# Zero blocks, lambda and position rows of the mixers' later parts, made behind the projection of the scan's inputs

## The chip, the cores and the metric

The kernel runs on one core of one Trainium2 chip. The metric is the device time of one execution in microseconds (us), as the median of several runs. The core has five engines that run their own queues in order and wait for each other by semaphores: PE (TensorE, matrix products), DVE (VectorE), ACT (ScalarE), POOL (GpSimd) and SP (SyncE, which here only issues DMAs). TensorE's granted clock has two levels, 1.2 and 2.4 GHz; the profile gives it as a share of the higher one.

## The reference, cut to what matters

Two request batches of 1024 rows and 1024 columns go through the same hybrid layer. One input projection feeds two mixers:

- Mixer A (RWKV-7): from columns r, k, v and three small groups (decay, learning rate, gate) comes a scan over time in both directions, with a matrix state of 64 x 64 for each of eight heads.
- Mixer B (differential attention): four heads with two halves each. The scores get a relative-position bias from a table of 32 buckets, and the second half's softmax is subtracted with a learned factor:

```
lam  = exp(sum(lp[0] * lp[1])) - exp(sum(lp[2] * lp[3])) + lam_init
attn = p[:, :, 0] - lam * p[:, :, 1]
```

The outputs of both are joined, projected, normalised, and go through a gated feed-forward part with a convolution of width three. All of it is float32; the dense products are made of three products of split values (a high and a low part of each operand).

## The kernel before

One core does both batches, and one program order is turned into five engine queues by a scheduler: each instruction has a priority (its place in the program, moved by the code), and of the instructions whose operands would be ready the scheduler takes the one of the best priority. The queues are fixed when the program is built; the chip only runs them.

`run` (L1138 on) lays the work out. The head is `consts`, the input norm of batch 0 (`norm_in`, with transposes into the two resident arrays `xh` and `xl`) and `columns`, which loads small parameters as rows and turns them into columns. Up to here priorities are the program's own. Then the dense code follows at a priority lowered by 100000: `project(0)` (14 column blocks of the input projection: block 12 with decay and rate, block 13 with the gate, then r, k, v for each of four pairs of heads), `project_qk(0)`, `project_v(0)`, `scan(0)`, then the same for batch 1, and the output and feed-forward parts. One column block is 48 products of 128x512 ("dense products" below: lines L264, L265, L266, and L288 to L290 for blocks in the other orientation). Beside `project(0)` and `project_qk(0)` the input norm of batch 1 runs (`between`).

`scan` stands late in the program but has a better priority (`self.first`) than all dense code, so its instructions go into the queues as soon as they can. It has three stages. `pass1` makes the scan's operands in 16 units (four pairs of heads, two halves of time, two directions): a decay product on PE (L549), tanh on ACT (L551), a running sum on DVE (L557), exponentials on ACT (L560, L562), the operand tile `AB` on DVE and POOL (L575, L576, L586, L587), a product of 32 small pieces on PE (L580), and stores. Every four units a triangular inversion runs on DVE (L619, L621, 30 pairs of small instructions), and two merges of its quarters run on PE (L647, L653) with copies on ACT, through DRAM scratch `td`. `pass2` is the chain of the scan itself (L724), and `attention` comes last. While `scan(0)` runs, the dense products of `project(1)` are released by its progress (`paced`), 50 us of them at once.

What the change touches stands at the end of `columns` (L195 to L226):

- the scratch `td` gets its zero blocks: a zero tile `zt` (DVE, L197) and eight DMAs from it (L201, issued by SP, each 1024 pieces of 128 bytes);
- lambda: a load, two DVE instructions (L206, L209), an exponential on ACT (L210), one DVE instruction (L211), one product on PE into a PSUM tile `pl` (L213), and a copy to `lamn` (L215);
- the position rows: a load of the bias table, 31 copies on POOL (L222), and two DMAs into the scratch `frow` (L225, L226).

`td` is read by `pass2` and written by `pass1`'s inversions; `lamn` and `frow` are read by `attention`. All small tiles come from the tag `t` (7 buffers), and `pl` comes from `spsum`, which hands out two tags, "a" and "b", in turn, each with two buffers:

```
def spsum(self, tag=None):
    self.side = not self.side
    return self.ps.tile([P, 512], F32, name=self.nm("s"), tag=tag or "ab"[self.side])
```

The tiles of a tag are handed out in the order in which the program asks for them. `pass1` asks for its products' tiles by the same function.

Of the kernel before, what the change touches and what calls it, by code (L numbers as in the profile page):

```python
# [42 lines left out]
class Trunk:  # L43
# [90 lines left out]
    def columns(self):  # L134

        nc, cp, I = self.nc, self.cp, self.I
# [55 lines left out]
        self.cb = cols[:, 300:344]  # L192
        self.rk = cols[:, rows["r_k"] : rows["r_k"] + 4]
        self.WC = self.cs.tile([P, NPAIR, 2, NC2, 2], F32, name="WC")
        self.td = [[self.scr(f"td{g}{h}", [P, 2, 2, NC2, C]) for h in range(2)] for g in range(2)]  # L195
        zt = self.dt("t", shape=(32, 4 * NC2, 32))
        nc.vector.memset(zt, 0.0)  # L197
# [940 lines left out]
    def run(self, x0, x1, y0, y1):  # L1138
        self.st = {}
        with self.tc.tile_pool(name="cs", bufs=1) as self.cs:  # L1140
            self.consts()
            for _ in self.norm_in(0, x0, True):
                pass
            self.columns()
            self.first_loads = self.loaded
            self.urgent = self.tc.cur_priority
            self.front = self.urgent + 30000
            self.first = self.urgent + 50000
            self.tc.cur_priority += 100000
            between = self.norm_in(1, x1)  # L1150
            self.project(0, between)
            self.project_qk(0, between)
            for g in range(2):
                turn = self.turn_in(1, g)
                next(turn)
                self.project_v(0, g)
                with self.ahead():
                    next(turn, None)
            self.scan(0)
            self.project(1)  # L1160
            self.project_qk(1)
            self.project_v(1, 0)
            self.project_v(1, 1)
            self.scan(1)
            with self.ahead():
                self.phase_o(0)
            self.phase_f1(0)
            self.phase_f2(0, y0)
            with self.tc.tile_pool(name="o1", bufs=1) as pool:
                self.phase_o(1, pool)  # L1170
        with self.tc.tile_pool(name="f1", bufs=1) as pool:
            h = pool.tile([P, KF, 2, 512], F32R, name="h")
            self.phase_f1(1, h)
            self.phase_f2(1, y1, h)
# [25 lines left out]
```

## Time and profile before

| | us |
|---|---|
| median of 3 runs (3603.18 to 3615.9) | 3606.48 |
| the profiled execution | 3613.08 |
| its span | 3611.3 |
| PE busy | 3254.0 (90%) |
| DVE busy | 1961.5 (54%) |
| ACT busy | 1379.4 (38%) |
| POOL busy | 1292.2 (36%) |

The span runs from the first to the last instruction that the profile shows; 1.8 us of the execution lie around it. A busy share is a mean over stages. In the timeline a row is one or several equal instructions: start, length, engine, line, operation, tiles; in square brackets the idle time of the engine before it and what ended that. A stretch of the span is written A:B, in us from its start.

### The profile page before, as it was taken

Reading aid. Unit: us, or ns where it says so; the run is one execution under the profiler, and the core shown is the slowest. Engines: PE = TensorE matmul, PEld = TensorE weight load, DVE = VectorE, ACT = ScalarE, POOL = GpSimd, SP = SyncE. Lnnn points to the kernel's source line nnn. Section 1 sums busy time; section 2 is a strip of 40 time slices with the busy share of each in tenths; the row PEclk is TensorE's granted clock in tenths of the full one; section 3 lists DMA queues with packets and bytes.
Section 4 is the critical chain, followed back from the end, with each engine's and each line's share of the span. In section 5 each row is a group of like instructions: output and inputs, shape, how many; then the busy total and the mean of one; then the engine's idle time right before and its main releaser. Section 6 shows DMA issues by size and latency. Waiting matters only on the chain. (4 is left out here: it accounts for less than half of the span.)

```text
span 3611.3 us, 56096 instructions
## 1 busy us (share of the span) xinstructions
PE 3254.0 (90%) x21477; PEld 2584.8 (72%) x21477; DVE 1961.5 (54%) x3550; ACT 1379.4 (38%) x2349; POOL 1292.2 (36%) x1387
## 2 busy tenths in 40 slices
PE   5788888998999986789999999989987899999997
PEld 4566666676777874567777787767865688888876
DVE  6378873335557866888534445366685633333022
ACT  3233332443245643345334343334454422332222
POOL 5365441001422445544121112363352622222464
PEclk9898888998999998788999999999999999999999
DMA  5568774534455655567543336586552322222642
GB/s 161 163 201 228 211 193 126 154 106 118 128 171 155 215 200 165 162 153 166 127 133 115 117 104 210 175 261 209 185 188 93 114 71 71 70 70 70 225 172 87
DMA packets 603360, 545.59 MB, mean 151 GB/s; under 512 B 205341, under 2 KB 477965, under 8 KB 603093
## 3 DMA queue, kind: packets, MB, share of 16 engines
q1 hardware_dynamic: 536532, 508.44, 46.3%
q10 hardware_dynamic: 66560, 33.56, 3.9%
q8 instruction: 171, 2.80, 0.3%
q14 instruction: 97, 0.79, 0.1%
HBM read 361.49 MB, written 180.39 MB: 150 GB/s over the span
## 5 line engine op out<-in xcount | busy, mean ns | idle before, releaser
L251 POOL TENSOR_TENSOR w<-w,whi 128x256 fp32r<-128x256 f32 (+1 forms) x800 | 758.6, 975 | 1246.1 <-ACT whi L248 1088.0
L264 PE MATMUL d<-xh,whi 128*128 128x512 f32 (+1 forms) x2112 | 863.7, 409 | 17.8 <-DVE t L399 6.0
L265 PE MATMUL d<-xl,whi 128*128 128x512 f32 (+1 forms) x2112 | 855.2, 405 | 0.6 <-DVE xl L308 0.6
L266 PE MATMUL d<-xh,w 128*128 128x512 f32 (+1 forms) x2112 | 853.7, 404 | 2.1 <-POOL w L251 2.1
L248 ACT ACTIVATE whi<-w 128x512 fp32r<-128x512 f32 (+1 forms) x536 | 307.9, 622 | 728.7 <-PE d L290 234.5
L264 PEld LDWEIGHTS d<-xh,whi 128*128 128x128 f32 (+1 forms) x2112 | 408.7, 194 | 117.3 <-issue 8.8
L266 PEld LDWEIGHTS d<-xh,w 128*128 128x128 f32 (+1 forms) x2112 | 407.9, 193 | 99.7 <-POOL w L251 3.3
L265 PEld LDWEIGHTS d<-xl,whi 128*128 128x128 f32 (+1 forms) x2112 | 408.2, 193 | 93.5 <-issue 2.0
L1071 DVE SCALAR_TENSOR_TENSOR t<-d,cols,t 128x1023 f32<-128x1023 f32 x88 | 112.8, 1282 | 455.7 <-ACT t L1070 442.6
L288 PE MATMUL d<-whi,xh 128*128 128x512 f32 x640 | 259.2, 413 | 31.5 <-DVE t L1051 15.1
L289 PE MATMUL d<-w,xh 128*128 128x512 f32 x640 | 259.2, 405 | 0.9 <-POOL w L251 0.9
L290 PE MATMUL d<-whi,xl 128*128 128x512 f32 x608 | 245.7, 404 | 0.0
L1051 DVE SCALAR_TENSOR_TENSOR t<-t,d 128x512 f32<-128x512 f32 x112 | 72.7, 678 | 244.7 <-PE d L290 240.7
L928 ACT ACTIVATE e<-e,ms 128x1024 f32<-128x1024 f32 x128 | 147.1, 1149 | 123.8 <-DVE ms L926 105.3
L935 POOL TENSOR_SCALAR e<-e,ms 128x512 f32<-128x512 f32 x128 | 88.1, 701 | 268.8 <-DVE ms L933 110.7
L288 PEld LDWEIGHTS d<-whi,xh 128*128 128x128 f32 x640 | 123.9, 194 | 66.7 <-DVE rs L1051 11.9
L739 DVE TENSOR_TENSOR G<-s,ms 64x256 f32<-64x256 f32 x128 | 53.4, 417 | 171.4 <-PE s L724 170.3
L289 PEld LDWEIGHTS d<-w,xh 128*128 128x128 f32 x640 | 124.0, 194 | 29.5 <-POOL w L251 2.2
L290 PEld LDWEIGHTS d<-whi,xl 128*128 128x128 f32 x608 | 117.2, 193 | 28.3 <-issue 1.0
L919 PE MATMUL s<-k,qh 128*128 128x512 f32 x256 | 113.9, 446 | 25.9 <-DVE ms L922 15.6
L619 DVE TENSOR_TENSOR Ntmp<-N 128x30 f32<-128x30 f32 (+14 forms) x240 | 111.3, 464 | 34.0 <-DMA N<-abd 29.0
L758 POOL COPY vr<-v 128x256 f32<-128x256 f32 x32 | 13.0, 405 | 324.4 <-DMA v<-va 311.3
(228 smaller groups left out, 5944.9 us busy)
## 6 DMA issues: line engine op xcount, KB each, us to landing
w<-in_ffn_up SPq DMA_DIRECT2D x88, 512.0 KB
w<-in_ffn_down SPq DMA_DIRECT2D x88, 512.0 KB
h<-t SPq DMA_DIRECT2D x66, 512.0 KB
ab<-AB ACTq DMA_DIRECT2D x64, 512.0 KB
w<-in_w_in SPq DMA_DIRECT2D x58, 512.0 KB
G<-ab SPq DMA_DIRECT2D x128, 128.0 KB
BK<-ab SPq DMA_DIRECT2D x64, 256.0 KB
w<-in_w_out SPq DMA_DIRECT2D x32, 512.0 KB
```

The lines of the kernel that those rows point to most:

```text
L248: nc.scalar.activation(out=hi[:, s], in_=w[:, s], func=AF.Copy)
L251: nc.gpsimd.tensor_tensor(out=lo[:, s], in0=w[:, s], in1=hi[:, s].bitcast(F32), op=ALU.subtract)
L264: nc.tensor.matmul(o, wh, rh, start=first, stop=False)
L265: nc.tensor.matmul(o, wh, rl, start=False, stop=False)
L266: nc.tensor.matmul(o, wl, rh, start=False, stop=last)
L288: nc.tensor.matmul(out[i], lh, wh, start=k == ks[0], stop=False)
L289: nc.tensor.matmul(out[i], lh, wl, start=False, stop=False)
L290: nc.tensor.matmul(out[i], ll, wh, start=False, stop=k == ks[-1])
L619: nc.vector.tensor_tensor(out=tv, in0=N[:, 0:j, j : j + 1].to_broadcast([P, j, w]), in1=N[:, j : j + 1, j + 1 : 32].to_broadcast([P, j, w] ...
L919: nc.tensor.matmul(pp, q_[0], k_[c][:, ks], start=True, stop=False)
L928: nc.scalar.activation(out=e_, in_=e_, func=AF.Exp, bias=ms[:, 2 + c : 3 + c], accum_out=ms[:, 4 + c : 5 + c])
L1071: nc.vector.scalar_tensor_tensor(out=o[:, 1:T], in0=pp[:, 0 : T - 1], scalar=self.cw[0][:, m : m + 1], in1=o[:, 1:T], op0=ALU.mult, op1=AL ...
```

## The change

The three groups at the end of `columns` become a function of their own, `tables`, with the same instructions, and `run` calls it behind `project(0)` instead of within `columns`. In the program they now stand behind `project(0)` and ahead of `project_qk(0)`, at the dense code's priority.

```diff
         self.WC = self.cs.tile([P, NPAIR, 2, NC2, 2], F32, name="WC")
+
+    def tables(self):
+
+        nc, cp, I = self.nc, self.cp, self.I
         self.td = [[self.scr(f"td{g}{h}", [P, 2, 2, NC2, C]) for h in range(2)] for g in range(2)]
         zt = self.dt("t", shape=(32, 4 * NC2, 32))
         nc.vector.memset(zt, 0.0)
...
             self.project(0, between)
+            self.tables()
             self.project_qk(0, between)
```

All five queues change from the head on until the first steps of `pass2` of batch 0. From about the 3000th of PE's 16822 products on, each engine's queue holds the same instructions in the same order as before.

On PE, before, at lambda's product (`s_419`; `d_544` is block 13, `d_624` block r of pair 0):

```order
L264 MATMUL d_544<-xh,whi_536 96x512
L265 MATMUL d_544<-xl,whi_536 96x512
L266 MATMUL d_544<-xh,w_537 96x512
L213 MATMUL s_419<-t_415,bcol 128x1
L264 MATMUL d_624<-xh,whi_616 128x512
```

Lambda's product stood here between blocks 13 and r, and the first decay product of `pass1` (`s_2584`) 43 rows further, within block r.

On PE, now, at the same two products (lambda's is `s_1478`; `d_1628` is the first k block of `project_qk(0)`, `stk_273` are the loaded decay rows):

```order
L269 MATMUL d_1628<-xl,whi_1620 128x512
L270 MATMUL d_1628<-xh,w_1621 128x512
L217 MATMUL s_1478<-t_1474,bcol 128x1
L553 MATMUL s_2584<-stk_273_2549,up_262_2521 128x512
L268 MATMUL d_1628<-xh,whi_1620 128x512
```

Both moved from within `project(0)` to the second block of `project_qk(0)`: 723 dense products now stand ahead of them, where 96 stood ahead of lambda's and 138 ahead of the decay product; the decay product asks for its tile next after lambda's in the same tag.

On SP, before, at the end of `columns` and in the first blocks of `project(0)` (`w` are weights, `stk` the decay and rate rows):

```order
L79 DMA td_401<-t_402 1024x1x32 x2
L79 DMA t_412<-in_lam 1x256
L79 DMA kk_2532<-in_iclr_up 128x1x512
L79 DMA kk_2539<-in_iclr_up 128x1x512
L79 DMA t_423<-in_rel_bias 4x32x1
L79 DMA frow<-t_425 4x1024
L79 DMA w_678<-in_w_in 128x8x128
L79 DMA stk_529<-t_525 4x32x1024 x2
L79 DMA stk_529<-t_526 4x32x1024 x2
L79 DMA frow<-t_426 4x1023
```

Here the weights `w_678` and the `stk` stores stood behind all of the zero blocks, lambda's load and the first half of the position rows.

On SP, now, at the same place:

```order
L79 DMA kk_2532<-in_iclr_up 128x1x512
L79 DMA kk_2539<-in_iclr_up 128x1x512
L79 DMA w_615<-in_w_in 128x8x128
L79 DMA w_679<-in_w_in 128x8x128
L79 DMA stk_466<-t_462 4x32x1024 x2
L79 DMA stk_466<-t_463 4x32x1024 x2
L79 DMA t_536<-in_g_up 96x512
L79 DMA stk_273_2549<-stk_466 128x512
```

The zero blocks, lambda's load and the position rows have left this place; the next weights and the `stk` stores follow the two loads of `in_iclr_up` directly. They stand again some fifty rows later, between the loads for the first blocks of `project_qk(0)`.

## Rows read from the trace of the kernel before

**Rows 1.** The page's first part: busy time of each engine.

```profile
PE 3254.0 (90%) x21477; PEld 2584.8 (72%) x21477; DVE 1961.5 (54%) x3550; ACT 1379.4 (38%) x2349; POOL 1292.2 (36%) x1387
```

**Rows 2.** Busy time by stretch: length, each engine's busy us, clock, DMA share, GB/s.

```profile
66.70:107.70 41.00, 13.61 (x45) 10.14 (x44) 11.49 (x14) 5.91 (x7) 13.18 (x39) 0.68 0.33 106
...
148.16:313.17 165.01, 147.04 (x738) 115.71 (x736) 124.80 (x172) 57.34 (x81) 92.50 (x93) 0.91 0.69 206
313.17:509.94 196.77, 162.23 (x1236) 128.07 (x1237) 151.80 (x241) 81.18 (x114) 95.86 (x88) 0.83 0.79 215
509.94:632.50 122.56, 102.52 (x908) 82.44 (x906) 47.66 (x88) 34.11 (x49) 27.39 (x40) 0.87 0.56 134
```

**Rows 3.** Timeline of PE in the head: end of block 13 and two gaps.

```profile
66.34 0.40 PE L266 MATMUL d<-xh,w 128*96 128x512 f32 x1
...
76.16 0.76 PE L264 MATMUL d<-xh,whi 128*128 128x512 f32 x1 [6.04 <-DVE t L399]
...
107.72 0.79 PE L549 MATMUL s<-stk,up 128*128 128x512 f32 x1 [16.59 <-DMA stk<-stk]
```

**Rows 4.** Timeline of SP's queue in the head.

```profile
54.29 7.95 SPq L79 DMA_DIRECT2D td<-t  x8
...
75.73 0.25 SPq L79 DMA_DIRECT2D frow<-t  x1
76.08 0.40 SPq L79 DMA_DIRECT2D w<-in_w_in  x1
78.28 7.27 SPq L79 DMA_DIRECT2D stk<-t  x4
...
104.34 1.77 SPq L79 DMA_DIRECT2D stk<-stk  x4
```

**Rows 5.** Timeline of POOL in the head: the position rows' copies.

```profile
71.71 6.64 POOL L222 COPY t<-t 4x1 f32<-4x1 f32 x31 [18.52 <-DMA t<-in_rel_bias]
```

**Rows 6.** Timeline of PE in undisturbed dense work, 60 products apart.

```profile
113.03 0.40 PE L265 MATMUL d<-xl,whi 128*128 128x512 f32 x1
...
127.03 0.40 PE L265 MATMUL d<-xl,whi 128*128 128x512 f32 x1
```

**Rows 7.** PE's groups by line, 100:640, the gate's products.

```profile
L426 PE MATMUL d<-t,t 96*128 96x512 f32 x17 | 8.3, 604 | 1.5 <-ACT t L428 1.5
```

**Rows 8.** Timeline of DVE: L576 of units 1, 2, 7 and 16.

```profile
148.16 0.68 DVE L576 TENSOR_TENSOR AB<-ta,sg 128x512 f32<-128x512 f32 x1
...
158.71 1.69 DVE L576 TENSOR_TENSOR AB<-ta,sg 128x512 f32<-128x512 f32 x1
...
313.17 0.68 DVE L576 TENSOR_TENSOR AB<-ta,sg 128x512 f32<-128x512 f32 x1
...
509.94 1.68 DVE L576 TENSOR_TENSOR AB<-ta,sg 128x512 f32<-128x512 f32 x1
```

**Rows 9.** What PE waited for in 148:513: us, times, longest.

```profile
PE s L580 <- DVE AB L576: 24.6, 9, 5.1
```

**Rows 10.** Timelines of DVE, SP and PE: last inversion, last merges, first products of `pass2`.

```profile
562.75 0.19 DVE L621 TENSOR_TENSOR N<-N,Ntmp 128x30 f32<-128x30 f32 x1
577.91 2.21 PE L647 MATMUL s<-M,A 32*32 32x32 f32 x64
...
584.85 2.21 PE L653 MATMUL s<-M,A 32*32 32x32 f32 x64
...
588.98 9.79 SPq L79 DMA_DIRECT2D A<-abd  x1
598.86 3.22 SPq L79 DMA_DIRECT2D td<-M  x1
...
608.06 3.59 PE L647 MATMUL s<-M,A 32*32 32x32 f32 x64 [11.88 <-DMA M<-t1d]
...
619.87 2.21 PE L653 MATMUL s<-M,A 32*32 32x32 f32 x64
...
632.52 1.16 PE L724 MATMUL s<-G,BK 64*128 64x128 f32 x16
```

## The prediction

> **What bounds the kernel now.** I read the busy shares first: PE is busy for 90% of the span [rows 1], so a microsecond counts only where PE stands idle or at the low clock. Then I read the queues' order before and after. Behind about the 3000th product on PE all five queues are the same as before, so the whole effect is decided ahead of that, and what I need is one time: when `pass2` of batch 0 starts. Before it is 632.5 us [rows 10]. What follows is carried along unchanged. So I read only the stretches up to there [rows 2]. Three things are to be seen.
>
> In the head (66.7 to 107.7) PE works 13.6 of 41.0 us at a mean clock of 0.68 [rows 2]. Two gaps make that: 6 us until 76.16, where block r waits for the evacuation of block 12 (DVE L399), and 16.6 us until 107.72, where the first decay product waits for the decay rows to come back from DRAM [rows 3]. Behind both stands SP, which issues one DMA after the other: eight zero-block stores take it 7.95 us, then the position rows hold it until 75.7 while POOL's 31 copies wait 18.5 us for the bias table and take 6.6 us [rows 4, 5]. The next weights are issued only at 76.08 and the `stk` stores at 78.28 [rows 4]. The table code is on the path of the head.
>
> In `pass1` (148 to 510) PE is not short of work, it waits in order for DVE: 24.6 us at the 32 small products of L580 for the `AB` tile [rows 9]. From unit 7 on all inputs are there, and nine units take 196.8 us, 21.9 each [rows 8], with DVE busy 151.8 us, 77% [rows 2].
>
> In the tail (510 to 632.5), from the last unit through the last inversion and four merges to `pass2`, PE still has dense work to fill in: 276 dense products stand there, counted in the order.
>
> **The change, part by part.** I work in times of the profiled execution (3613.08 us), and add the result to the median of 3606.48, which is 6.6 lower.
>
> *The head gets free.* The zero blocks no longer stand ahead of the two `in_iclr_up` loads whose DVE work precedes L399; they go out 7.95 us earlier [rows 4]. PE's 76.16 less that is 68.2; block 13's products end at 66.7 [rows 3], so block r starts at about 69. Weights of the next blocks and the `stk` stores are no longer behind the position rows. In the same order the first product that needs decay rows stands behind 240 dense products, not 138.
>
> *What is moved behind it, and what it holds.* Lambda's product now stands behind 723 dense products, and the first decay product directly behind it. Its own operands have long been there, but its tile is asked for after lambda's. So unit 1 of `pass1` waits for nearly all of `project(0)`: that is the added wait, and behind it stand all 16 units, since every unit's `AB` follows the one before on DVE. Until there PE does 723 - 96 = 627 dense products at 14.00/60 = 0.233 us [rows 6], 146 us, and eight gate products of 0.6 us, 5 us [rows 7], with three products of `pass1`, 2 us. 69 + 153 = 222. Nothing of `pass1` makes PE wait in this stretch, and where PE was undisturbed before it did not wait for weights. From the decay product to unit 1's `AB` I take 7 us (the chain through tanh, running sum and exponentials); that gives unit 1 at 229, where before it was at 148.2 [rows 8]. Zero blocks, lambda and copies themselves lie beside dense work; on SP their 8 us of issues stand ahead of a weight load that is needed some 20 us later, and on POOL their 6.6 us end about when unit 1 needs POOL. I cost them at nothing; without that cover it would be the 8 us.
>
> *Pass 1 without waiting for inputs.* Before, unit 1 to unit 16 took 361.8 us [rows 8], in part because r, k and v came only as `project(0)` made them. Now all are there, but much of the dense work that used to lie beside it is done already. From unit 1 to 16 the new order has 701 dense products in 15 steps, 47 a step; units 7 to 16 before had 423 in nine, also 47. The same mix is the nearest row, so I take 21.9 us a step. Only the first three steps have no inversion beside them; the first step ran before in 158.71 - 148.16 = 10.5 us [rows 8], and I take 47 us for the three, with the longer step between pairs. 47 + 12 x 21.9 = 310, unit 16 at 539, which is 29 us later than 509.9. The ends: 15 x 21.9 = 329 above; below, DVE's own work of 151.8/9 = 16.9 a step [rows 2] at 90% instead of 77%, 18.7 x 15 = 281. So unit 16 lies between 510 and 558.
>
> *The tail gets shorter.* 122.6 us before [rows 2]. From the last inversion's end (562.9) to `pass2` it took 69.6 us [rows 10], because the `stk` stores and gate weights of `project(1)` stood in SP's queue: one load was held 9.8 us and one store 3.2 us [rows 10], and between the last two groups of merges PE took 11.8 us (608.06 to 619.87) where the step before took 6.9 (from 577.91 to L653 at 584.85). In the new order these stores stand ahead of unit 14, and behind unit 16 there are 18 dense products instead of 276. I take off 12 for SP, 5 for the merge behind dense work, and 4 for the rest: 21. It could be 10 (PE then runs the merges at the low clock) or 28. That PE stands idle here costs nothing more: its work was done earlier.
>
> *A lead.* When `pass2` starts, 1485 dense products are done, not 1463: 22 x 0.233 = 5 us less to do later.
>
> **Sum:** +29 - 21 - 5 = +3 us: 3606.48 + 3 = 3609. About 26 us of idle PE in the head go, and the same comes back as `pass1` that starts 81 us later and has less dense work to hide behind. With the ends: 0 - 28 - 5 = -33 to +48 - 10 = +38.
>
> **The rivals.**
>
> *A: pass 1 catches up.* If the units go as fast as DVE's work allows, unit 16 stands at 510, as before, and the tail and the lead remain: 0 - 21 - 5 = -26, 3580 us. For it: DVE waited before for ACT and inputs, and its order now has the starts of later units further ahead. Against: even with all inputs there, steps were 21.9 us.
>
> *B: pass 1 pays, and the tail too.* The late start is a stall of the whole scan: at 21.9 us for every step, unit 16 is at 558 (+48), and the stalled SP queue of the `stk` stores now falls within `pass1` instead of the tail, so only 10 to 14 come off there: +34, 3640 us. It decides from unit 16 later than about 550. For it: two instructions of L576 on equal tiles took 0.68 and 1.69 us [rows 8], and DVE's steps lengthen when packed; POOL is busy 95.9 of 196.8 us in units 7 to 16 [rows 2]. Against: the early steps have no inversion.
>
> The Trainium skill bears on this (page "SBUF — State Buffer", section "Who interferes with whom"): a DVE instruction with two inputs in SBUF and a GpSimd instruction that reads SBUF use one shared port pair as an exclusive lock, and the second waits until the first has ended. The two lengths of L576 fit that, though no row shows which POOL instruction stood beside. By that rule packing the units tighter buys collisions, and the time would be B's, 3640, not 3609.
>
> *C: the head does not get free.* The `stk` stores needed from 78.28 to 104.34 until the loads behind them went out [rows 4], 26 us. If they need the same from about 71, the loads go out at 97 and the next weights behind them; should PE stand there for 12 us, everything is 12 later: 3621.
>
> **How the numbers follow.** About 0.3%, 11 us, is what a measurement of this kernel can tell from no change. The forecast has 0.40 (of it 0.07 faster by more, 0.27 within, 0.06 slower: its own spread is 15 us either way, 3594 to 3624). A has 0.30, all faster. B has 0.23, slower. C has 0.07, 0.03 within and 0.04 slower. Faster 0.37, within 0.30, slower 0.33. The range goes from just below A to B: 3577 to 3640.
>
> **What would show it.** Right: no gap of PE from 76 to 108 and full clock from 69 on; lambda's product near 222; L576's (now L580) first at 229 and sixteenth at 525 to 550; some 100 us from there to the first product of `pass2`, at 635 to 640, with PE mostly idle; everything behind shifted by one constant. A is shown by a sixteenth unit before 515, B by one behind 550 with a tail of 110 or more, C by a gap of PE ahead of the first rate product. The prediction is wrong in kind if what follows `pass2`'s start does not shift by a constant, or if PE waits for weights in `project(0)`.

## The result, and the profile after

The changed kernel takes 3642.57 us (median of 4 runs, 3641.98 to 3644.44), the kernel before in the same comparison 3609.53. The ratio is 1.0095, with a 95% interval of 1.0079 to 1.0111: it is slower by 33 us, where 3609 was forecast. The profiled execution took 3644.44 us, 31.4 more than the one of before.

The work itself is the same, as the page's first part shows; it answers to [rows 1].

```profile
PE 3252.4 (89%) x21477; PEld 2586.5 (71%) x21477; DVE 1956.5 (54%) x3550; ACT 1379.7 (38%) x2349; POOL 1294.2 (36%) x1387
```

The stretches of the changed kernel up to `pass2`, in the columns of [rows 2]: from block r to the end of the gate, from there to lambda's product, units 1 to 7, units 7 to 16, and the tail.

```profile
77.64:137.93 60.29, 49.09 (x164) 33.75 (x165) 14.94 (x13) 18.91 (x23) 13.56 (x18) 0.80 0.45 147
137.93:249.00 111.07, 111.07 (x485) 90.68 (x484) 51.62 (x65) 29.79 (x41) 46.63 (x54) 1.00 0.55 169
...
258.76:381.57 122.81, 101.04 (x555) 77.28 (x555) 87.86 (x123) 45.53 (x65) 77.96 (x97) 0.92 0.78 229
381.57:585.41 203.84, 150.68 (x1209) 116.71 (x1208) 149.51 (x243) 84.33 (x119) 86.78 (x80) 0.80 0.73 188
585.41:667.34 81.93, 41.98 (x625) 37.66 (x624) 27.94 (x71) 13.13 (x20) 8.68 (x16) 0.61 0.48 92
```

For 111 us PE does nothing but dense products at the full clock. Then that work is missing: in the tail PE is busy for half of the time and its mean clock is 0.61, where it was busy for 84% at 0.87 before [rows 2].

Timeline of PE at the places that decide (start, length, engine, line, operation; in brackets the idle time before it): block 13, block r, the last product ahead of the gate, the gate, the first dense product behind it, lambda's product with the first decay product, and the first product of `pass2`.

```profile
61.80 0.80 PE L269 MATMUL d<-xl,whi 128*128 128x512 f32 x1 [4.95 <-DVE xl L312]
...
77.64 0.56 PE L268 MATMUL d<-xh,whi 128*128 128x512 f32 x1 [2.22 <-ACT whi L252]
...
112.04 0.40 PE L270 MATMUL d<-xh,w 128*128 128x512 f32 x1
120.16 3.75 PE L430 MATMUL d<-t,t 96*128 96x512 f32 x4 [7.71 <-issue]
126.95 2.07 PE L543 MATMUL s<-L,bones 128*128 128x512 f32 x2 [3.04 <-ACT L L541]
...
137.93 0.80 PE L268 MATMUL d<-xh,whi 128*128 128x512 f32 x1
...
249.00 0.38 PE L217 MATMUL s<-t,bcol 1*128 1x1 f32 x2
249.31 0.50 PE L553 MATMUL s<-stk,up 128*128 128x512 f32 x1
...
667.34 1.01 PE L728 MATMUL s<-G,BK 64*128 64x128 f32 x6 [7.78 <-DMA BK<-ab]
```

The decay product runs right behind lambda's, at 249; in the kernel before it ran at 107.72 [rows 3]. `pass2` starts at 667.34, in the kernel before at 632.52 [rows 10]: 34.8 us later.

Timeline of DVE, the instruction L580 (L576 before) of units 1, 4, 7 and 16; it answers to [rows 8].

```profile
258.76 0.68 DVE L580 TENSOR_TENSOR AB<-ta,sg 128x512 f32<-128x512 f32 x1
...
318.18 1.67 DVE L580 TENSOR_TENSOR AB<-ta,sg 128x512 f32<-128x512 f32 x1
...
381.57 0.68 DVE L580 TENSOR_TENSOR AB<-ta,sg 128x512 f32<-128x512 f32 x1
...
585.41 1.68 DVE L580 TENSOR_TENSOR AB<-ta,sg 128x512 f32<-128x512 f32 x1
```

Unit 1 starts 110.6 us later than before; units 1 to 16 take 326.6 us in place of 361.8, and the tail 81.9 in place of 122.6: 110.6 - 35.2 - 40.7 = 34.7 us.

What PE waited for between block r and `pass2` (us in total, times, longest):

```profile
PE s L651 <- DMA M<-t1d: 49.0, 5, 16.8
PE s L584 <- DVE AB L580: 40.0, 9, 8.5
PE d L430 <- issue: 7.7, 1, 7.7
```

In the kernel before, between the same two places, it waited 13.7 us for the merges' loads (L647) and 24.6 for `AB` [rows 9]. PE's idle time from 61.8 on shows where the time went: ahead of unit 1 it fell from 31 us to 13, not by the 26 that were forecast; from unit 1 to unit 16 it grew from 53 to 75, and in the tail from 20 to 40. By what ended the waits, it is 35 us more at the merges, 20 of them in the tail where little dense work is left, and 15 more at `AB`.

### The profile page after: what moved, and what is told of

Same layout as the page of the kernel before. It is cut to its first block, busy times and chain, and to the rows that moved or that the text cites. A ratio compares the mean times of both kernels' runs of the same rounds, so it can differ in the third digit from the quotient of the medians.

```text
span 3642.7 us, 56123 instructions
## 1 busy us (share of the span) xinstructions
PE 3252.4 (89%) x21477; PEld 2586.5 (71%) x21477; DVE 1956.5 (54%) x3550; ACT 1379.7 (38%) x2349; POOL 1294.2 (36%) x1387
## 5 line engine op out<-in xcount | busy, mean ns | idle before, releaser
L269 PE MATMUL d<-xl,whi 128*128 128x512 f32 (+1 forms) x2112 | 843.9, 400 | 5.6 <-DVE xl L312 5.6
L270 PE MATMUL d<-xh,w 128*128 128x512 f32 (+1 forms) x2112 | 844.2, 400 | 0.4 <-POOL w L255 0.4
L728 PE MATMUL s<-G,BK 64*128 64x128 f32 x1024 | 107.5, 306 | 27.4 <-DMA BK<-ab 7.8
```

Source lines behind the costliest of these rows:

```text
L269: nc.tensor.matmul(o, wh, rl, start=False, stop=False)
L270: nc.tensor.matmul(o, wl, rh, start=False, stop=last)
L728: last = self.nc.tensor.matmul(*args, **kw)
```

## The experiments

In all of them "before" is timed on the same chip. A variant is told by which of the three groups stays in `columns` and which goes into `tables`. Counts of dense products in the expectations include the eight gate products (731 there is 723 in the prediction); the 119 of e10's is 120 in the queues' order. The table gives each kernel's milestones from its trace, the dense products done when `pass2` starts against the kernel before (from the queues' order), and the result.

| kernel | unit 1 | unit 16 | `pass2` | dense | median | ratio to before, 95% interval |
|---|---|---|---|---|---|---|
| before | 148.2 | 509.9 | 632.5 | 0 | 3604 to 3610 | 1 |
| changed | 258.8 | 585.4 | 667.3 | +22 | 3642.57 | 1.0095, 1.0079 to 1.0111 |
| e1, lambda alone moved | 253.6 | 568.1 | 668.3 | +22 | 3642.02 | 1.0103, 1.0076 to 1.0130 |
| e2, zero blocks alone | 139.6 | 496.7 | 610.2 | -52 | 3599.49 | 0.9980, 0.9966 to 0.9994 |
| e3, lambda in other PSUM | 143.6 | 497.3 | 603.5 | -120 | 3621.74 | 1.0047, 1.0032 to 1.0062 |
| e4, lambda stays | 137.3 | 496.0 | 629.1 | -9 | 3616.21 | 1.0038, 1.0023 to 1.0052 |
| e5, lambda half way | 184.2 | 507.4 | 623.7 | +22 | 3610.43 | 1.0020, 1.0005 to 1.0035 |
| e6, lambda later | 341.7 | 642.7 | 727.3 | +22 | 3713.15 | 1.0299, 1.0269 to 1.0329 |
| e7, casts behind `xl` | 250.3 | 575.3 | 656.4 | +22 | 3636.41 | 1.0091, 1.0058 to 1.0124 |
| e8, e2 and weights first | 136.1 | 495.6 | 611.3 | -52 | 3594.53 | 0.9972, 0.9958 to 0.9986 |
| e9, e8 with two queues | 136.8 | 495.8 | 607.0 | -52 | 3597.58 | 0.9968, 0.9953 to 0.9982 |
| e10, e3 with ACT's queue | 143.4 | 495.8 | 606.8 | -120 | 3612.94 | 1.0011, 0.9999 to 1.0022 |
| e11, e8 with two weights | 132.6 | 492.8 | 624.8 | -9 | 3597.06 | 0.9972, 0.9956 to 0.9988 |
| e12, smaller k, r, E1 | 256.3 | 572.4 | 648.5 | +22 | 3624.80 | 1.0051, 1.0033 to 1.0069 |
| e13, e12 with two `AB` | 258.2 | 560.0 | 649.7 | +22 | 3597.50 | 0.9972, 0.9957 to 0.9986 |
| e14, before with two `AB` | 146.4 | 489.6 | 620.4 | -9 | 3581.86 | 0.9940, 0.9921 to 0.9958 |
| e15, e8 with two `AB` | 135.3 | 480.6 | 606.0 | +19 | 3558.88 | 0.9877, 0.9856 to 0.9898 |

### What holds pass 1

e1 moves lambda alone:

```diff
-        pl = self.spsum()
-        nc.tensor.matmul(pl[:, 0:1], self.bcol[0:1, 4:5].to_broadcast([1, P]), l1, start=True, stop=True)
...
+    def tables(self):
...
+        pl = self.spsum()
+        nc.tensor.matmul(pl[:, 0:1], self.bcol[0:1, 4:5].to_broadcast([1, P]), l1, start=True, stop=True)
...
             self.project(0, between)
+            self.tables()
```

> Only lambda is moved behind the projection; zero blocks and position rows stay in columns. Its product and the first decay product again stand behind 727 to 731 dense products, where 96 and 138 stood before. Theory (lambda's PSUM tile holds pass 1): unit 1 of pass 1 at about 250 to 260, as in the changed kernel, and 3635 to 3645 us. Rival (the loss comes from the head, where the moved zero blocks and position rows let the casts of in_iclr_up, the weights and the stk stores come at another time): the head is that of the kernel before, and so is the time, 3605 to 3615 us.

3642.02 us, the whole loss of the change, with zero blocks and position rows in the head as before (block r at 77.03). Its decay product again runs right behind lambda's (246.8), and unit 1 stands at 253.62:

```profile
253.62 0.68 DVE L581 TENSOR_TENSOR AB<-ta,sg 128x512 f32<-128x512 f32 x1
...
668.26 1.01 PE L729 MATMUL s<-G,BK 64*128 64x128 f32 x6 [7.95 <-DMA BK<-ab]
```

e3 is the changed kernel with one line different, the pool that lambda's tile comes from:

```diff
-        pl = self.spsum()
+        pl = self.dpsum()
```

> The whole change, with lambda's product written to a tile of the dense products' PSUM pool in place of a tile that pass 1 asks for next. Lambda's product still stands behind 680 dense products, the first decay product behind 166. Theory: pass 1 starts at 125 to 140, the head's faster dense work is kept, pass 2 starts earlier than 632 and the time is below the kernel before, 3580 to 3603 us. Rival (moving the three groups costs by itself, through SP, DVE or POOL): 3630 to 3645 us as in the changed kernel.

Lambda's product is still late (303 us), but unit 1 stands at 143.61, 115 us earlier than in the changed kernel. That shows the hold: it is the tile. (As lambda no longer asks `spsum`, the two tags of all later tiles swap as well; each tag is still handed out in the order of the program.) The time, 3621.74, lies between the two expectations. `pass2` starts at 603.53, but with 120 dense products fewer done, which is 120 x 0.23 = 28 us, and then PE waits 14 us for a load of v:

```profile
143.61 0.68 DVE L582 TENSOR_TENSOR AB<-ta,sg 128x512 f32<-128x512 f32 x1
...
603.53 0.72 PE L730 MATMUL s<-G,BK 64*128 64x128 f32 x8
...
637.38 0.45 PE L767 MATMUL s<-ident,v 128*128 128x128 f32 x1 [14.15 <-DMA v<-va]
```

That load stands on SP behind the `stk` stores of `project(1)`, which fall within the first steps of `pass2` here. e10 is e3 with these stores on ACT's queue:

```diff
-            self.ld(out=S["stk"][:, g], in_=(lh, ll)[g % 2])
+            self.ld(out=S["stk"][:, g], in_=(lh, ll)[g % 2], eng=nc.scalar if b == 1 else None)
```

> As e3 (the whole change, lambda in the other PSUM pool), and the stk stores of project(1), which in e3 stand on SP within the first steps of pass 2, are issued by ACT. Behind them the queues differ in places from those of e3. Theory (e3 lost 14.2 us because pass 2 waited for v behind these stores): that wait is gone and the time is 3604 to 3612 us. Rival (e3 is slow because 119 dense products fewer are done when pass 2 starts): 3617 to 3625 us.

3612.94, and in the same stretch of the trace the waits for v are down to 4.4 us. Against the kernel before, e3 lost 16 us and e10 loses 5, and its interval takes in 1: about two thirds of the loss went with the stores. The wait went mostly, not wholly, and the time ended just above the range of the theory.

e4 leaves lambda's lines in `columns` and moves the two other groups. Against the changed kernel:

```diff
     def columns(self):
...
+        lp = self.dt("t", shape=(1, 6, 64))
...
     def tables(self):
...
-        lp = self.dt("t", shape=(1, 6, 64))
```

> Zero blocks and position rows are moved, lambda stays in columns. The first decay product stands behind 166 dense products; behind the 3500th product the queues differ from those of the kernel before. Theory: as e3, 3580 to 3605 us, give or take 10 for the other order behind. Rival (the head pays): 3620 to 3645 us.

3616.21, between the ranges. Unit 1 is early (137.3), as the theory said, but the tail is 133 us long, and PE's queue is that of the kernel before in its last 3547 of 16822 products only (the expectations of e4 and e11 mean this count, which is from the end). So it can't be told from e4 what moving the position rows is worth.

e5 and e6 are e1 at two other points: the call stands within `project`, behind its second pair of heads, or behind `project_qk`.

```diff
             if p == 0:
                 gate()
+            if p == 1 and b == 0:
+                self.tables()
```

> As e1, but lambda is made half way through the projection: its product and the first decay product stand behind 427 dense products (96 and 138 before, 731 in e1). Theory (the delay of pass 1 costs only as far as it outlasts the wait for r, k and v that units 3 to 6 had anyway): unit 1 at about 190, 42 us later than before, unit 7 at 300 to 315 as before, and 3595 to 3615 us. Rival (the cost is in proportion to the delay): 36 us for 105 us in e1, so about 15 for 42, 3620 us.

> As e1, but lambda is made behind project_qk: its product stands behind 1110 dense products in place of 731, which is 379 x 0.229 = 87 us later. Theory (every microsecond of delay counts from here on, since the dense work that would cover it is done already): unit 1 at 335 to 345 and 3700 to 3735 us. Rival (the loss is that of moving lambda at all, or pass 1 gets shorter by as much when it has DVE and POOL for itself): 3635 to 3670 us.

Both times lie in the ranges of the theory. With unit 1 at 184.2, 36 us late, unit 7 stands at 308.2 (313.2 before [rows 8]), and the time is 3610.43. With unit 1 at 341.7 it is 3713.15. From the kernel before to e5 a delay of 36 us costs about 5 us; from e1 to e6 another 88 us cost 71, and `pass2` comes 59 us later. So not every microsecond counts, as the theory had it, but four of five: units 1 to 16 (301.0 us in place of 314.5) and the tail (84.6 in place of 100.1) make good a part. Pass 1 could start late as long as its third to sixth unit would have waited for r, k and v; beyond that most of it is paid. (These two have other queues behind, too, as e4.)

### What the head cost

e2 moves the zero blocks alone. Against the kernel before:

```diff
-        zt = self.dt("t", shape=(32, 4 * NC2, 32))
-        nc.vector.memset(zt, 0.0)
...
+    def tables(self):
...
+        zt = self.dt("t", shape=(32, 4 * NC2, 32))
+        nc.vector.memset(zt, 0.0)
...
             self.project(0, between)
+            self.tables()
```

> Only the zero blocks are moved; lambda and position rows stay in columns. The first decay product stands behind 168 dense products. Theory: pass 1 starts at 125 to 150, and the time is that of the kernel before or better, 3585 to 3612 us. Rival (the head pays): on DVE the casts of in_iclr_up stand ahead of the last xl tiles as in the changed kernel, PE waits there 5 us and the stk stores hold SP, so that 10 to 30 us are lost, 3620 to 3640 us.

3599.49, 6 us less than before, and the interval just leaves out 1. Block r starts at 71.7, pass 1 9 us earlier. So the rival is out: the head does not pay for the zero blocks.

e7 is the changed kernel with the casts of `in_iclr_up` put behind the last `xl` tile of batch 0.

```diff
+                with self.tc.issue_after(self.first_low.ins) if b == 0 else nullcontext():
-                nc.vector.tensor_copy(out=up[0:64], in_=raw[0:64])
-                nc.vector.tensor_copy(out=tmp[64:128], in_=raw[64:128])
+                    nc.vector.tensor_copy(out=up[0:64], in_=raw[0:64])
+                    nc.vector.tensor_copy(out=tmp[64:128], in_=raw[64:128])
```

> The changed kernel, with the casts of in_iclr_up put behind the last xl tiles on DVE, as before the change. Theory (the 5 us that PE waited for xl, and the low clock behind it, make block r start at 77.6 in place of 69, and lambda and pass 1 come as much later): block r at 69 to 71, unit 1 at 249 to 252, and 3632 to 3638 us. Rival (the stk stores and the weights behind them take the gain back at once): unit 1 at 257 to 260 and 3640 to 3645 us.

Timeline of PE, block r and the gate:

```profile
70.42 0.47 PE L270 MATMUL d<-xh,whi 128*128 128x512 f32 x1 [3.06 <-DVE t L405]
...
113.32 3.75 PE L432 MATMUL d<-t,t 96*128 96x512 f32 x4 [9.68 <-issue]
```

Block r starts 7.2 us earlier, the gap ahead of the gate takes 2 of them back, and unit 1 is 8.5, `pass2` 11 us earlier. The trace shows the term; the median of 3636.41 agrees with it, but its interval takes in the changed kernel's time.

e8 is e2 with one load of weights ahead of the loads of the decay and rate rows on SP.

```diff
+                        with self.tc.issue_after(self.wl[5].ins) if b == 0 and n == 0 else nullcontext():
-                        self.ld(out=st, in_=S["stk"][j, :, :, 256 * n : 256 * n + 512]...)
+                            self.ld(out=st, in_=S["stk"][j, :, :, 256 * n : 256 * n + 512]...)
```

> As e2 (only the zero blocks moved), and one load of weights is put ahead of the loads of the decay and rate rows on SP's queue; the first decay product stands behind 181 dense products, 168 in e2. Theory (in the head PE waits because these loads wait for their stores and hold the weights behind them): the wait of 16 us at the first decay product falls to 13 or less and no wait for weights comes after it; 3 to 8 us less than e2, 3591 to 3597 us. Rival (pass 1 sets the start of pass 2, and dense work that is done earlier is waited for later): as e2, 3599 us, or slower.

e9 is e8 with two of the four `stk` stores issued by ACT:

```diff
-            self.ld(out=S["stk"][:, g], in_=(lh, ll)[g % 2])
+            self.ld(out=S["stk"][:, g], in_=(lh, ll)[g % 2], eng=nc.scalar if b == 0 and g % 2 else None)
```

> As e8, and two of the four stk stores of batch 0 are issued by ACT in place of SP. Theory (SP's own queue is what the stores fill): the loads of the decay and rate rows go out 5 us or more earlier than in e8, PE's wait of 14.7 us at the first decay product falls below 10, and the time is 3 to 8 us below e8, 3586 to 3592 us. Rival (the stores land no sooner, whichever engine issues them): the wait stays at 13 to 15 us and the time at 3593 to 3597 us.

and e11 is e8 with two loads of weights first:

```diff
-                        with self.tc.issue_after(self.wl[5].ins) if b == 0 and n == 0 else nullcontext():
+                        with self.tc.issue_after(self.wl[6].ins) if b == 0 and n == 0 else nullcontext():
```

> As e8, with two loads of weights ahead of the loads of the decay and rate rows, and the first decay product behind 229 dense products (181 in e8). Behind the 3500th product the queues differ from those of the kernel before. Theory: PE's wait at the first decay product, 14.7 us in e8, falls below 6 us; 5 to 10 us less than e8, 3585 to 3590 us, give or take 10 for the other order behind. Rival (pass 1 starts later by as much, so pass 2 does too): 3594 to 3605 us.

e8, e9 and e11 all lie at 0.997 and can't be told apart. e8's time is in the theory's range, but the wait at the first decay product is 14.7 us where 13 or less was expected. In e9 SP's weights leave 6.5 us earlier, but the loads of the rows still leave at 102.77 (101.40 in e8), and PE waits 16.0 us; wait and time lie just above the rival's ranges, and nothing of the theory came. What PE waited for, and the timeline of SP:

```profile
PE s L556 <- DMA stk<-stk: 16.0, 1, 16.0
```

```profile
75.37 1.16 SPq L79 DMA_DIRECT2D stk<-t  x2
76.63 1.73 SPq L79 DMA_DIRECT2D t<-in_g_up  x1
81.93 0.39 SPq L79 DMA_DIRECT2D w<-in_w_in  x1
102.77 0.35 SPq L79 DMA_DIRECT2D stk<-stk  x1
```

In e11 the wait is 8.1 us, where less than 6 was expected, and the time is e8's. Unit 1 is 3.5 us earlier, `pass2` 13.5 us later with 43 products more done; its queues behind are not e8's, so it doesn't say why.

### What sets the pace of pass 1

e12 takes one buffer each from k, r and E1; e13 gives the room to a second buffer for `AB`.

```diff
-                            x[key] = tl(key, 3 if key in "kr" else 1)
+                            x[key] = tl(key, 2 if key in "kr" else 1)
...
-            E1 = tl("E1", 2, shape=(P, NC2, C + 1))
+            E1 = tl("E1", 1, shape=(P, NC2, C + 1))
...
-            AB = tl("AB", 1, shape=(P, NC2, 4, C))
+            AB = tl("AB", 2, shape=(P, NC2, 4, C))
```

> The changed kernel with two buffers in place of three for k and r, and one in place of two for E1; the comparison for e13. Theory and rival alike: steps of pass 1 as in the changed kernel or up to 2 us longer, 327 to 357 us from unit 1 to unit 16, 3640 to 3675 us.

> As e12, with two buffers for AB in place of one. Theory (the stores of AB set the pace of pass 1, 55 us of waits in 15 steps): the waits of DVE and POOL for the stores of AB fall to 10 us or less together and unit 1 to 16 takes 20 to 45 us less than in e12. Rival (the chain of a unit through DVE, ACT and PE sets it, and the waits for the stores only hide others): within 8 us of e12, with longer waits of DVE for ACT or PE.

e12 surprised: 3624.80, at 1.0051 of the kernel before where the changed kernel is at 1.0095, some 16 us less, with a tail of 76 us. Its PE queue, too, is that of the other kernels in the last 3547 products only, and I have no cause for it. Against it, e13's units take 301.8 us in place of 316.1, 14 us less: between the theory's 20 and the rival's 8. The waits for the stores of `AB`, 22.1 us of DVE and 25.4 of POOL in e12, are gone; POOL's waits for ACT at one line, the product kd, grew from 25.0 to 68.0 (at all its lines together from 103 to 121). And `pass2` starts no earlier (649.7 and 648.5), since the tail is 14 us longer. The 27 us by which e13 is faster come behind it.

e14 makes the same three edits in the kernel before, e15 in e8.

> The kernel before with two buffers for AB (and one buffer less for k, r and E1, as in e13). Theory (the second buffer's gain is in batch 1 and independent of where lambda is made): 3604 less 20 to 30 = 3574 to 3584 us or lower. Rival (the gain is that of the late start alone, which the second buffer makes good): 3595 to 3610 us.

> e8 (only the zero blocks moved, one load of weights first) with two buffers for AB as in e13. Theory (the two add up): e8's 10 us less and e14's 20 to 30 us less than the kernel before, 3565 to 3578 us. Rival: the early start of pass 1 is worth nothing beside the second buffer, as e14.

The second buffer is worth 23 us in the kernel before (3581.86), as the theory said, though not in batch 1 alone: `pass2` of batch 0 starts 12 us earlier. With e8's early start the time is 3558.88 us, 46 less than before and below the range of 3565 to 3578: the two gains, 10.5 and 23 us, add up, and 12 us come on top that no run here explains. At 0.9877 of the kernel before it is the fastest version here.

## Why the prediction was wrong

**Right: where it is decided.** `pass2` starts 34.8 us later with 22 dense products more done (5.1 us): 29.7 us, and the profiled execution is 31.4 us longer. In the kernels whose PE queue behind is that of before, this account (delay of `pass2`, less 0.23 us for each dense product more) comes out near the measured difference: e2 -10 for -6, e8 -9 for -11, e9 -14 for -10, e1 +31 for +37; e3 -1, and +13 with the wait for v, for +16. For e7 it is +19 for +31, where its runs scatter from 3627 to 3661. In e4, e5 and e6, with other queues behind, the time is 12 to 20 us above the account; that part is not explained.

**Right: what is held and by what.** Lambda's product and the first decay product run in that order 0.3 us apart, and e3 and e1 show the tile as the cause. The trace fits: unit 1's products in the other tag were not held, its rate product ran at 128.03 and the decay product of its other direction at 132.68.

**Wrong: the head gets free (69), lambda near 222.** It ran at 249.00, 27 us later. Three terms make that.

- Block r started at 77.64, 8.6 us late. With the zero blocks gone from SP, the loads of `in_iclr_up` go out early, and so the scheduler had put their casts on DVE ahead of the last two `xl` tiles, which I had not looked for. Timeline of DVE:

```profile
60.17 0.42 DVE L491 CAST up<-kk 64x512 fp32r<-64x512 f32 x1 [5.89 <-DMA kk<-in_iclr_up]
60.60 0.42 DVE L492 CAST sg<-kk 64x512 fp32r<-64x512 f32 x1
61.06 0.69 DVE L312 TENSOR_TENSOR xl<-s,xh 128x512 fp32r<-128x512 f32 x1
```

PE stood 4.95 us for that tile and then ran at the low clock, 0.63 us a product, until 67.5. e7 takes this term away.

- PE stood 7.71, 3.04 and 0.44 us at the gate, 11.2 in all. That is rival C, which I had at 12 us and a chance of 0.07, and by the prediction's own sign (PE waits for weights in `project(0)`) it is an error in kind. The 7.71 us are ended by nothing that the profile names, but a chain fits them: ACT stands 22.80 us for weights, so it is late with block k, whose evacuation on DVE (L403) ends at 120.05, and the gate's first product starts at 120.16. Timelines of SP's queue, and of ACT and DVE:

```profile
80.27 7.54 SPq L79 DMA_DIRECT2D stk<-t  x4
87.86 5.00 SPq L79 DMA_DIRECT2D t<-in_g_up  x1
106.35 1.79 SPq L79 DMA_DIRECT2D stk<-stk  x4
108.18 0.43 SPq L79 DMA_DIRECT2D w<-in_w_in  x1
...
238.87 7.60 SPq L79 DMA_DIRECT2D td<-t  x8
246.57 0.97 SPq L79 DMA_DIRECT2D w<-in_w_in  x1
```

```profile
115.27 1.15 ACT L252 ACTIVATE whi<-w 128x512 fp32r<-128x512 f32 x2 [22.80 <-DMA w<-in_w_in]
```

```profile
118.77 1.28 DVE L403 SCALAR_TENSOR_TENSOR t<-d,cols,t 128x1023 f32<-128x1023 f32 x1
```

From the first `stk` store to the loads of the rows it is 26.1 us, as in the kernel before [rows 4], and the weights wait behind them. Nothing in the new order shortened that; the chance was too small.

- The gate and the products of pass 1 beside it took 14.3 us, not 7 (25.5 us without a dense product, from 112.44 to 137.93, less the 11.2 of waits). I took eight gate products of 0.6 us; the row had 17 records of 604 ns, two for each product and one over, and 8.3 us of busy time at a better clock [rows 7].

8.6 + 11.2 + 7.3 = 27.1 us.

**Wrong: zero blocks and copies cost nothing.** From lambda's product to unit 1 it took 9.8 us, not 7. The stores hold SP from 238.87, the weights behind them leave at 246.57, and ACT stands 7.08 us at them, with the tanh of the decay product behind. Timeline of ACT:

```profile
253.22 1.16 ACT L252 ACTIVATE whi<-w 128x512 fp32r<-128x512 f32 x2 [7.08 <-DMA w<-in_w_in]
254.28 0.67 ACT L555 ACTIVATE sg<-s,halfc 128x512 f32<-128x512 f32 x1
```

In e1, where the zero blocks stay in the head, the same way takes 6.9 us (246.76 to 253.62). I had named the transfer and not what is queued behind the instruction that waits for it.

The copies of the position rows stand on POOL between unit 1's instructions. Timelines of POOL, of ACT, which issues the stores of `AB`, and of DVE at unit 2's first write of `AB`:

```profile
257.82 3.97 POOL L226 COPY t<-t 4x1 f32<-4x1 f32 x14
```

```profile
265.54 1.55 ACTq L79 DMA_DIRECT2D ab<-AB  x2
```

```profile
278.17 0.69 DVE L579 SCALAR_TENSOR_TENSOR AB<-kk,E 128x512 f32<-128x512 f32 x1 [8.71 <-DMA ab<-AB]
```

Unit 1's stores go out 6.8 us behind its L580, and DVE waits 8.71 us for them. In e1, where the copies stay in the head, they go out 3.0 us behind it, DVE waits 2.27 us, and the first step takes 17.3 us in place of 21.7. No run moves the copies alone, so their share isn't measured.

**Wrong in size: 310 us from unit 1 to 16.** It took 326.6, near the upper end of 329: the first three steps 59.4 us in place of 47, the others 22.3 each in place of 21.9. The step that failed is that units without an inversion beside them go at 15.7 us; they went at 19.8. In the trace two engines wait for the stores of the one `AB` tile (what DVE and POOL waited for, units 1 to 16):

```profile
DVE AB L579 <- DMA ab<-AB: 21.1, 4, 8.7
```

```profile
POOL AB L590 <- DMA ab<-AB: 34.1, 5, 11.2
```

Before it was 3.4 us of DVE and 12.4 of POOL. Of DVE's 21.1 us, 13.2 lie in the first three steps, about the 12.4 by which these are too long. With a second buffer (e13) they take 47.9 us, as forecast, but e12 has them at 55.4 with one buffer: the wait is shown for 7.5 us there, and for 14 of all 15 steps. What holds the rest is open. Units 7 to 16 take 194 to 204 us in the kernel before, the changed one and e1 to e9, whatever dense work lies beside.

**Wrong in size: a tail of 101 us.** It took 81.9. I had taken all 21 us off behind the last inversion. It ends at 629.80, 44.4 us behind unit 16 in place of 53.0, so 8.6 us came ahead of it, where I had taken nothing off; and from there to `pass2` it is 37.5 us in place of 69.6, 11 more than the 21. With next to no dense work left and no store of `stk` on SP, the merges follow each other faster than I allowed, though PE does a group of 64 in 3.4 us where it took 2.2 before [rows 10].

At `pass2`: 27.1 + 2.8 + 16.6 - 19.1 = 27.4 us above the forecast's 640. Rivals B and C were priced as if one of them would happen, but they add: C's wait came, and of B the long pass 1. With them came three terms that no rival had, the casts, the gate's size and the load behind the zero blocks (18.7 us together), and only the tail, shorter than any term had it, held the sum near the range. The sum's own ends went to +38, 3644, and hold 3642.57; the range was drawn at B, 3640.

**B came by half, and without its reason.** Pass 1 took nearly B's 329 us, but the tail, by B 110 us or more, took 81.9. By the Trainium skill (page "SBUF — State Buffer", section "Who interferes with whom") a DVE instruction with two inputs in SBUF and a GpSimd instruction that reads SBUF lock one port pair against each other. The trace agrees with the lock (below). I had made of it that denser units would collide more, and that did not come: L580 is longer than 1.1 us in 7 of 16 units now, and was in 10 of 16 before. DVE's busy time in units 7 to 16, which would hold such waits, is 149.5 us, and was 151.8 [rows 2]. Longer DVE instructions did not make these steps slow.

## What to carry over

Before an instruction is moved, look at whose turn its output tile takes: an order of buffers that is fixed by the program lets a product that nobody is waiting for hold a whole stage. A late start of the scan cost little as long as its later steps would have waited anyway (5 us for 36), and most of it beyond that (71 us for 88); so count what time the stage starts, and how much filling work is left by then. Rivals that sit at different places of the same chain add up, and the range must hold their sum.

## What the runs showed of the hardware

The two lengths of L576 and L580, 0.68 us or 1.1 to 1.8, go with what POOL does. Timelines of the changed kernel, DVE in unit 2, and POOL in units 2 and 16 (DVE's row of unit 16, 585.41, stands in the first section):

```profile
280.48 1.63 DVE L580 TENSOR_TENSOR AB<-ta,sg 128x512 f32<-128x512 f32 x1
```

```profile
279.86 1.71 POOL L570 TENSOR_TENSOR kd<-kd,k 128x512 f32<-128x512 f32 x1
...
584.74 1.80 POOL L570 TENSOR_TENSOR kd<-kd,k 128x512 f32<-128x512 f32 x1
```

The DVE instruction starts while POOL's runs, and ends 0.55 us behind POOL's end (281.57 and 282.11; 586.54 and 587.09), as if it waited and then did its own work. In all seven long cases of the changed kernel and all ten of the kernel before a TENSOR_TENSOR of POOL stood beside it. In the short cases POOL was idle, did a small fill or copy, or had a TENSOR_TENSOR that ended within 0.1 us of DVE's start or began with or behind DVE's.

With four stores of 512 KB it is 26 us from the first issue to the loads that wait for them, in the kernel before and after, and 27.4 when two engines issue two each (e9: 75.37 to 102.77). Who issues them did not change this time; only the queue behind them is relieved.
